# Seven block products for eight in half of an attention's input projection

## The chip, the cores and the metric

The kernel runs on one core of one Trainium2 chip. The core has five engines with instruction streams of their own: TensorE (PE, matmuls), VectorE (DVE), ScalarE (ACT), GpSimd (POOL) and SyncE (SP, which here only issues transfers). Sixteen DMA engines move data between the chip's memory and the core's buffers: SBUF (128 partitions) and PSUM (8 banks of 512 fp32 numbers for each partition, into which PE writes). The metric is the device time of one execution in microseconds.

## The reference

A diffusion step of two layers over 256 prompt tokens and 2048 sample tokens (a grid of 32 rows by 64 columns) of width 1024. Layer 0 is a convolution branch, layer 1 neighbourhood attention with 16 heads of 64:

```python
for i in range(DEPTH):                       # 2 layers
    shift, scale, gate = ada_params(c, ada_w[i], ada_b[i])
    h = modulate(x, norm_g[i], shift, scale) # RMS norm, scaled and shifted
    if i % 2 == 0:
        out = conv_branch(h, conv_w_in, conv_dw_w, conv_dw_b, conv_ln_g, conv_ln_b, conv_w_out)
    else:
        q, k, v, z = split(h @ na_w_in, 4)   # the input projection: 1024 x 4096
        att = attention(q, k, v, ...)        # prompt: its own keys; sample: 8 x 16 window + 512 cached keys
        out = (att * silu(z)) @ na_w_out
    x = x + gate * out
y = rms_norm(x, final_g)                     # also the prompt's k and v are outputs
```

Everything is fp32 in and out. The kernel keeps the accuracy by splitting each operand in a high and a low part in the PE's reduced format (hi = rounded, lo = rest) and adding three products: hi x hi, hi x lo and lo x hi.

## The kernel before

**Stages.** `conv_layer` runs layer 0's input projection and convolution; `conv_out_pipeline` and `conv_out` its output projection, tile by tile of 128 tokens, and store `x1_d`. Then layer 1's input projection goes in two sets of tokens: A (prompt 256, sample 0 to 767) and B (sample 768 to 2047, as blocks of 256, 512 and 512). `na_rest` makes q, k and z (`part` 0, 1, 3): one *pass* for each of 8 column tiles `ct` and 3 parts loads a weight of 1024 x 128, splits it (`halves`: ACT rounds, POOL subtracts) and multiplies each block of the set, 8 k-tiles by 3 matmuls (`project`, L362 to L364). `na_values` makes v with 256 columns a time, 128 tokens a time (L1009 to L1011). Results go to memory: `qh_d`, `ql_d`, `ks_d`, `vs_d`, `zn_d`. `phase2` is the attention of the sample tokens by units of a head, 512 queries and one of four column blocks (names `sa_`); it reads them back.

**Side work** that depends on no product is woven in among the passes: `context_keys` and `context_values` (cached keys and values split in parts), `masked_bias` (for 16 heads and 3 kinds of row, a tile of three slices, mask minus bias, stored to `bm_d`; DVE at L1105, store at L1106), `gated_weights` (the output weights times the gate, split), `prompt_attention`, `prompt_out`. `weave(main, side, n)` takes n side steps after each step of the main work:

```python
self.weave(self.na_values(B, lambda: next(rest)), side, 2)     # side: context keys, masked bias
self.weave(itertools.islice(rest, 13), side, 3.6)
...
self.weave(itertools.islice(rest, 6), side, 13)                # prompt attention, gated weights, context values
...
self.weave(itertools.islice(rest, 2), side, 18)                # prompt output
```

**Order.** In the convolution, and on PE and DVE in the attention, instructions stay in the program's order. In between, a planner orders each engine's instructions by a simulated timeline, with the program's order as priority; on the chip each engine then runs its own list in that fixed order and waits by semaphores. Tiles come from pools by tag with a number of buffers; a new tile waits until the last readers of its buffer are done. When a pool closes, its memory goes to a later pool, under the same rule.

**Hand-over.** The last passes of set B are interleaved by hand with the first scores of the attention (`self.begun`, banks in `s0`), whose loads `start_attention` issues earlier.

## Time and profile before

| what | value |
|---|---|
| median of 3 runs (lowest, highest) | 2794.38 us (2789.11, 2807.89) |
| the profiled execution | 2795.33 us |
| its span, first to last instruction | 2793.5 us |
| mean granted clock of TensorE in it | 0.992 |
| busy: PE, DVE, ACT, POOL | 2679.9, 1766.0, 1377.9, 1408.2 us |
| bytes moved | 533.86 MB, mean 191 GB/s |

In the profile's rows a tile is named as in the program with its numbers left out: `ni_s` is the PSUM bank of a pass over sample tokens, `nip_`/`nis_` weights of set A and B, `v_ps` and `wv_` those of the values, `h_s_hi` the high part of the input, `bm` a tile of the bias. L362 is a line of the kernel. "<-" after an idle time names what ended it. SPq is the queue of transfers that SP issues; a granted clock of 1.00 is full speed. Busy times of PE include the tails of overlapping matmuls. The stretches of the work: output of the convolution from about 745 us, passes of set A to 1220, values of set A to 1330, values of set B to 1441, passes of set B to 1826, the attention to the end.

### The profile page before, as it was taken

To read this page: it belongs to the slowest core of one execution; us is meant where nothing else is said; L and a number is where in the kernel's file an instruction comes from. 1 tells how busy PE (TensorE), PEld (TensorE's weight loads), DVE (VectorE), ACT (ScalarE), POOL (GpSimd) and SP (SyncE) were. 2 spreads that over 40 slices of the span, in tenths; PEclk is the share of its full clock that TensorE was granted. 3 is DMA by queue.
4 is the path that set the end of the run, shared out by engine and by line. 5 is a ranking of instruction groups with operands and counts; after the bars stand their busy time and mean duration, and the time that the engine had idled before them with its cause. 6 is when DMAs were issued, how large, how long until landed. Compare 5 with 4: busy or idle time off the path is not lost.

```text
span 2793.5 us, 45263 instructions
## 1 busy us (share of the span) xinstructions
PE 2679.9 (96%) x16081; PEld 2318.9 (83%) x16081; DVE 1766.0 (63%) x3052; ACT 1377.9 (49%) x2437; POOL 1408.2 (50%) x1589
## 2 busy tenths in 40 slices
PE   6999999999999999999999999988999999999998
PEld 4888877776777889999998888777888898888887
DVE  4678778888985510012556532468787787878885
ACT  4446454456453322234222244356676676667774
POOL 4687776567563343355123235244455555555564
PEclk9999999999999999999999999999999999999999
DMA  7233554556546554446789986588666767966652
GB/s 259 72 128 112 179 193 141 163 190 200 176 117 178 161 162 132 127 146 198 244 297 337 365 255 188 190 222 223 201 199 196 203 171 203 275 182 192 197 165 107
DMA packets 443833, 533.86 MB, mean 191 GB/s; under 512 B 77745, under 2 KB 320393, under 8 KB 443480
## 3 DMA queue, kind: packets, MB, share of 16 engines
q1 hardware_dynamic: 435568, 503.82, 59.7%
q10 hardware_dynamic: 6664, 22.82, 2.1%
q0 software_dynamic: 1376, 4.33, 0.4%
q8 instruction: 128, 2.10, 0.3%
q14 instruction: 97, 0.79, 0.1%
HBM read 355.14 MB, written 179.79 MB: 191 GB/s over the span
## 4 chain that ended last, share of the span: by engine, by line
PE 72%; DMA 10%; DVE 5%; POOL 3%; SPq 3%; ACT 3%; issue 3%; POOLq 0%; ACTq 0%; DVEq 0%
PE sa_T L1652 7%; PE ci_ps L362 6%; PE ci_ps L363 6%; PE ci_ps L364 6%; PE sa_O L1681 5%; PE sa_O L1676 4%; PE ni_s L362 4%; PE ni_s L363 4%; PE ni_s L364 4%; PE sa_S L1620 3%; PE sa_S L1619 3%; DMA bm_d<-bm 2%; PE o L1781 2%; PE o L1783 2%; PE o L1782 2%
## 5 line engine op out<-in xcount | busy, mean ns | idle before, releaser
L1646 POOL TENSOR_SCALAR sa_p<-sa_p,sa_m 128x992 f32<-128x992 f32 (+2 forms) x256 | 278.2, 1087 | 428.9 <-DVE sa_m L1645 291.7
L514 POOL TENSOR_TENSOR cv_p<-cv_p,cv_p 128x640 f32<-128x640 f32 (+1 forms) x240 | 359.7, 1499 | 118.7 <-ACT cv_p L511 105.8
L1661 ACT CAST sa_pt<-sa_T 128x512 fp32r<-128x512 f32 (+3 forms) x512 | 275.2, 588 | 207.9 <-PE sa_T L1652 194.5
L113 DVE TENSOR_TENSOR sa_pt<-sa_T,sa_pt 128x512 fp32r<-128x512 f32 (+3 forms) x512 | 328.4, 683 | 12.8 <-ACT sa_pt L1661 12.5
L362 PE MATMUL ci_ps<-h_s_hi,ci_wh 128*128 128x512 f32 x768 | 307.6, 400 | 9.1 <-ACT z L481 3.6
L364 PE MATMUL ci_ps<-h_s_hi,ci_wl 128*128 128x512 f32 x768 | 303.7, 395 | 0.0
L363 PE MATMUL ci_ps<-h_s_lo,ci_wh 128*128 128x512 f32 x768 | 303.7, 395 | 0.0
L1644 ACT ACTIVATE sa_p<-sa_S,sa_m 128x992 f32<-128x992 f32 (+2 forms) x256 | 267.3, 1044 | 66.8 <-DVE sa_m L1640 59.5
L1652 PE MATMUL sa_T<-ident,sa_p 128*128 128x128 f32 (+3 forms) x2048 | 272.9, 276 | 17.0 <-DVE sa_pt L113 16.9
L1652 PEld LDWEIGHTS sa_T<-ident,sa_p 128*128 128x128 f32 (+3 forms) x2048 | 237.6, 138 | 54.5 <-issue 14.8
L1638 DVE TENSOR_REDUCE sa_m<-sa_S 128x1 f32<-128x512 f32 x256 | 176.2, 688 | 146.3 <-PE sa_S L1620 133.4
L511 ACT ACTIVATE cv_p<-u,ws 128x640 f32<-128x640 f32 (+1 forms) x256 | 190.9, 777 | 134.7 <-DVE u L478 98.4
L534 DVE SCALAR_TENSOR_TENSOR cv<-u,dw,cv 128x640 f32<-128x640 f32 (+1 forms) x240 | 196.2, 817 | 0.5
L1681 PE MATMUL sa_O<-sa_pt,a_v 120*128 120x256 f32 (+5 forms) x1280 | 190.2, 278 | 0.0
L362 PEld LDWEIGHTS ci_ps<-h_s_hi,ci_wh 128*128 128x128 f32 x768 | 145.6, 190 | 49.1 <-ACT z L481 6.8
L534 DVE SCALAR_TENSOR_TENSOR cv<-cv_d,dw,cv 128x640 f32<-128x640 f32 (+1 forms) x224 | 182.8, 816 | 0.0
L1676 PE MATMUL sa_O<-sa_pt,cv 128*128 128x256 f32 x1024 | 174.9, 293 | 5.0 <-ACT sa_pt L1661 1.1
L1640 DVE CUSTOM_DVE_ANT_0 sa_S<-sa_S,a_bm,sa_m 128x480 f32<-128x480 f32 (+2 forms) x256 | 170.9, 668 | 11.3 <-DMA a_bm<-bm_d 2.4
L364 PEld LDWEIGHTS ci_ps<-h_s_hi,ci_wl 128*128 128x128 f32 x768 | 145.5, 189 | 33.6
L363 PEld LDWEIGHTS ci_ps<-h_s_lo,ci_wh 128*128 128x128 f32 x768 | 145.7, 190 | 31.1
L1681 PEld LDWEIGHTS sa_O<-sa_pt,a_v 120*128 120x128 f32 (+2 forms) x1280 | 166.8, 190 | 0.0
L362 PE MATMUL ni_s<-h_s_hi,nis_wh 128*128 128x512 f32 x384 | 150.3, 391 | 2.7 <-ACT ni_s_f L1047 2.4
(808 smaller groups left out, 7121.5 us busy)
## 6 DMA issues: line engine op xcount, KB each, us to landing
adaw<-in_ada_w SPq DMA_DIRECT2D x24, 1024.0 KB
ci_w<-in_conv_w_in SPq DMA_DIRECT2D x48, 512.0 KB
a_bm<-bm_d SPq DMA_DIRECT2D x32, 720.0 KB
x_s<-in_x_sample SPq DMA_DIRECT2D x32, 512.0 KB
vs_d<-v_s SPq DMA_DIRECT2D x128, 128.0 KB
a_qh<-qh_d SPq DMA_DIRECT2D x128, 128.0 KB
a_ql<-ql_d SPq DMA_DIRECT2D x128, 128.0 KB
a_v<-vs_d SPq DMA_DIRECT2D x32, 480.0 KB
```

The source lines that it names most:

```text
L113: self.nc.vector.tensor_tensor(out=lo, in0=src, in1=hi.bitcast(F32), op=ALU.subtract)
L362: self.nc.tensor.matmul(out, wh[:, k, :], hh[:, k, :], start=k == 0, stop=False)
L363: self.nc.tensor.matmul(out, wh[:, k, :], hl[:, k, :], start=False, stop=False)
L364: self.nc.tensor.matmul(out, wl[:, k, :], hh[:, k, :], start=False, stop=k == NK - 1)
L514: nc.gpsimd.tensor_tensor(out=st["t", 0], in0=st["t", 0], in1=st["t", j], op=ALU.add)
L534: nc.vector.scalar_tensor_tensor(out=st["acc", b], in0=d, scalar=w, in1=st["acc", b], op0=ALU.mult, op1=ALU.add)
L1644: nc.scalar.activation(p[:, n], S[:, n], AF.Exp, scale=-1.0, bias=m[:, 2:3], accum_out=m[:, 3:4])
L1646: nc.gpsimd.tensor_scalar(out=p[:, n], in0=p[:, n], scalar1=m[:, 3:4], scalar2=1.0, op0=ALU.mult, op1=ALU.mult)
L1652: nc.tensor.transpose(t[:w, c * P : c * P + P], p[:, x + c * w : x + c * w + w], self.ident)
L1661: nc.scalar.copy(pt[:w, 0, part, :, at], t)
L1676: nc.tensor.matmul(o, cv[:, c].rearrange("p s d -> p (s d)"), x, start=s + c == 0, stop=False)
L1681: nc.tensor.matmul(dst, v[:w, c0 + c].rearrange("p s d -> p (s d)"), loc[:, lo:hi], start=False, stop=s == 1 and c == 3)
```

## The change

Sample tokens 1024 to 2047 leave the pass scheme. Their input is one matrix, split in two halves of 512 tokens and two halves of 512 inputs; a pair of weight tiles is split likewise. The product of two 2 x 2 block matrices is made from seven block products (Winograd's form of Strassen's scheme) instead of eight, with sums of blocks before and after. The sums of input blocks are made once (`input_sums`: factors 11, T1, T2, 22, T3, 21, T4), the sums of weight blocks for each pair (`weight_sums`), the sums of products as they come (`combine`). `in_turn` makes weights ahead for `AHEAD` = 7 products (3 in the value groups).

The first set becomes prompt 256 and sample 0 to 1023, the last 256 of them as a *late block* of its own: it joins after the first value pass, and its passes for `ct` 0 and 1 and its first values come last (`end`). Prompt passes for `ct` 4 to 7 come first, alone (`alone`). All side work is put beside this set by `along`, which takes side steps by tokens done. The bias is stored slice by slice, its masks are kept in bf16; weight loads of the passes are issued by ACT, stores of the bias and the values by SP as before (the values' by ACT in the last group). Prompt output stays beside the block products. The attention begins after the last product, with nothing of it begun before.

```diff
+AHEAD = 7
+PARTS = 1, 0, 3
+BIAS_RATE = 2.0
+SIDE_RATE = 0.5
...
+    def along(passes, n, *sides):
...
+            for i, (side, rate) in enumerate(sides):
+                due[i] += rate * m / P
+                while due[i] >= 1:
+                    next(side, None)
+                    due[i] -= 1
...
+    def input_sums(self, blocks, pool, rows, h):
...
+        yield from rounded("11", b11, False)
+        yield from rest("11", b11)
+        yield from minus(b11, b12, b11)
+        yield from rounded("T1", b11, False)
+        yield from rounded("22", b22, True)
+        yield from minus(b12, b22, b12)
+        yield from rest("22", b22)
+        yield from minus(b22, b22, b11)
+        yield from rest("T1", b11)
+        yield from rounded("T2", b22, False)
+        yield from rounded("21", b21, True)
+        yield from rounded("T3", b12, False)
+        yield from rest("21", b21)
+        yield from minus(b21, b21, b22)
+        yield from rest("T2", b22, "b11")
+        yield from rest("T3", b12, "b22")
+        yield from rounded("T4", b21, False)
+        yield from rest("T4", b21, "b12")
...
+    def in_turn(self, groups):
+        todo = [(g, i) for g in groups for i in range(7)]
+        made, loaded, live = [], 0, 0
+        def load(upto):
+            nonlocal loaded
+            while loaded < min(upto, len(groups)):
+                next(groups[loaded]["w"])
+                loaded += 1
+        load(1)
+        for at, (g, i) in enumerate(todo):
+            while len(made) < len(todo):
+                j = len(made)
+                cost = todo[j][0]["cost"]
+                if j > at and live + cost > self.ahead:
+                    break
+                load(j // 7 + 1)
+                made.append(next(todo[j][0]["w"]))
+                live += cost
+                if j % 7 == 6:
+                    load(j // 7 + 2)
+            w, made[at] = made[at], None
+            g["product"](i, w)
+            live -= g["cost"]
+            yield
...
+        def put(f, i, half):
+            self.rest_out(cts[i], part, t0 + half * n, f, f"{nm}_{i}{half}")
+        def product(i, w):
+            pm = self.product_bank(f"{nm}_{i}")[:, :n]
+            wh, wl = w
+            hh, hl = h[FACTORS[i]]
+            for k in range(4):
+                nc.tensor.matmul(pm, wh[:, k, :], hh[:, k, :], start=k == 0, stop=False)
+                nc.tensor.matmul(pm, wh[:, k, :], hl[:, k, :], start=False, stop=False)
+                nc.tensor.matmul(pm, wl[:, k, :], hh[:, k, :], start=False, stop=k == 3)
+            tile = lambda tag: self.ws.tile([P, n], F32, tag=tag, name=f"{nm}_{tag}", bufs=2 if tag in ("s1", "u2") else 1)
+            self.combine(i, pm, kept, tile, put, scale)
+        kept = {}
+        return {"w": self.weight_sums(srcs, [P, 4, P], pool, nm), "product": product, "cost": 1}
...
+                t = kept["u2"] = tile("u2")
+                join(t, kept["s1"])
+                u4 = kept["u4"] = tile("u4")
+                nc.gpsimd.tensor_tensor(out=u4, in0=t, in1=kept["s5"], op=ALU.add)
+            elif i == 3:
+                join(kept["u4"], kept["u4"])
+            elif i == 4:
+                u3 = kept["u2"]
+                join(u3, u3)
+                nc.gpsimd.tensor_tensor(out=kept["s5"], in0=kept["s5"], in1=u3, op=ALU.add)
+            elif i == 5:
+                join(kept["s1"], kept["s1"])
+            else:
+                join(kept["u2"], kept["u2"])
+        done = {3: ("u4", 0, 1), 4: ("s5", 1, 1), 5: ("s1", 0, 0), 6: ("u2", 1, 0)}.get(i)
+        if done:
+            put(kept.pop(done[0]), *done[1:])
...
+    def masked_bias(self, heads, bufs, rows):
...
             nc.sync.dma_start(raw, self.bias_rows(h))
             for gk, G in enumerate((0, 1, 3)):
                 r0, R = KEY_ROWS[G]
                 view = lambda ap: ap[:, : 32 * R].rearrange("p (a r c) -> p a r c", a=4, c=CW)
-                t = work([P, 3, 480], "bias", 3, f"bm{gk}_{h}")
                 for i, cb in enumerate((16, 8, 0)):
+                    t = work(f"bm{gk}{i}_{h}")
                     bv = self.windows(raw, b0 * BIAS_COLS + cb, R)
-                    nc.vector.tensor_tensor(out=view(t[:, i]), in0=view(masks[gk][:, i]), in1=bv, op=ALU.subtract)
-                nc.sync.dma_start(self.bm_d[h, gk, :, :, : 32 * R], t[:, :, : 32 * R])
-                yield
+                    nc.vector.tensor_tensor(out=view(t), in0=view(masks[:, gk, i]), in1=bv, op=ALU.subtract)
+                    nc.sync.dma_start(self.bm_d[h, gk, :, i, : 32 * R], t[:, : 32 * R])
+                    yield
...
+            own = [(part, ct, A[:], "a") for part in PARTS for ct in range(2)]
+            alone = [(part, ct, A[:1], "p") for ct in range(4, NK) for part in PARTS]
+            first = own[:1] + [x for i in range(1, 6) for x in (own[i], *alone[2 * i - 2 : 2 * i])] + alone[10:]
+            values = [("v", c, A if c else A[:], "a") for c in range(4)]
+            then = [(part, 2 * pair + i, A if pair < 3 else A[1:], "+") for pair in (1, 2, 3) for part in PARTS for i in range(2)]
+            then = [(part, ct, A if ct < 4 else A1, "+") for part, ct, _, _ in then]
+            last = []
+            todo = first + values + then
+            end = [(part, ct, last, "+l") for part in PARTS for ct in range(2)] + [("v", 0, last, "l")]
+            products = self.passes(todo + end)
+            self.along(products, len(first), (out, 0.22))
+            for _ in out:
...
+                side = self.layer1_block(*late_block)
+                self.along(products, 1, (side, 0.8))
                 for _ in side:
                     pass
+                A.append(late_block)
+                A1.append(late_block)
+                bias = self.masked_bias(range(NH), 4, self.xp)
+                side = itertools.chain(self.context_keys(), self.gated_weights(), self.context_values())
+                beside = (bias, BIAS_RATE), (side, SIDE_RATE)
+                self.along(products, 3, *beside)
+                pq = prompt.enter_context(tc.tile_pool(name="pq", bufs=2, side="right"))
+                pqs = prompt.enter_context(tc.tile_pool(name="pqs", bufs=1, space=bass.MemoryType.PSUM, side="right"))
+                pa = map(bool, self.prompt_attention(pq, pqs))
+                self.along(products, 12, *beside, (pa, 0.22))
+                for _ in itertools.chain(bias, side):
+                    pass
+            hbf = c.enter_context(tc.tile_pool(name="hbf", bufs=1))
+            with tc.tile_pool(name="extra2", bufs=1) as xp:
+                self.xp = Tagged(xp, {"ln": 5})
+                side = self.input_rows(FIRST_SUMMED, hbf, blocks)
+                self.along(products, 1, (pa, 0.3))
+                self.along(products, 5, (pa, 0.3), (side, 1.25))
+                for _ in itertools.chain(side, pa):
+                    pass
+            prompt.close()
+            late.close()
+            right = lambda name: tc.tile_pool(name=name, bufs=1, side="right")
+            quarters = c.enter_context(ExitStack())
+            hb = quarters.enter_context(right("hb"))
+            self.xp = None
+            side = self.input_sums(blocks, hb, hbf, summed)
+            self.along(products, None, (side, 2))
+            for _ in side:
+                pass
...
+            more.close()
+            self.more = None
+            banks.close()
...
+                self.pm[:] = [(pool, bufs)]
+            self.ahead = AHEAD
+            with ExitStack() as s:
...
+                products = self.in_turn(self.rest_sums((FIRST_SUMMED, summed), self.x2))
+                side = self.prompt_out(po, pps)
+                self.weave(itertools.islice(products, 7), side, 0)
+                self.weave(products, side, 0.85)
...
+                self.ws = s.enter_context(tc.tile_pool(name="wv", bufs=1))
+                product_banks(s, "pv", 3)
+                products = self.in_turn(self.value_sums((FIRST_SUMMED, summed), self.x2))
+                for _ in range(4):
+                    next(products)
+                self.tail = True
+                for _ in products:
+                    pass
+            quarters.close()
             self.start_attention()
...
-            self.more = self.s0 = None
+            self.first_loads()
 
 
```

`input_rows` reads `x1_d` again, normalises and transposes it into the blocks b11, b12, b21, b22. `weight_sums` loads the two (values: four) weight tiles, gives high and low parts of a11, s1 = a21 + a22, s2 = s1 - a11, s4 = a12 - s2, s3 = a11 - a21, a12, a22 in this order; ACT rounds, POOL subtracts (DVE for s4, in the value groups for s2 and s3 too). `rest_out` splits q and k and stores them with z. Loads of the first two heads are issued by `first_loads` after the last products in the program's order, those of their values and gates by `load_rest` in the attention.

More of the change, by code (lines that the diff above doesn't have):

```diff
@@ L79, in __init__ @@
         self.ctx = ctx
[L80 removed]
         self.tail = False
[L82 removed]
+        self.pm, self.turn, self.later = [], 0, []
+        self.more, self.more_turn = None, 0
+        self.prompt_tiles = 0
         self.cp = ctx.enter_context(tc.tile_pool(name="consts", bufs=1))
@@ L966, in spread_bias, with rest_sums, value_sums @@
+    def rest_sums(self, block, pool):
+        todo = [(pair, part) for pair in range(NK // 2) for part in PARTS]
+        return [self.rest_group(*block, pair, part, pool) for pair, part in todo]
+    def value_sums(self, block, pool):
+        return [self.value_group(*block, g, pool) for g in range(2)]
     def spread_bias(self):
@@ new lines, in values @@
+    def values(self, _, c, w, src, t0, n, hi, lo):
+        nc = self.nc
+        wh, wl = w
+        for s in range(0, n, P):
+            pm = self.mm_bank(f"v_ps{c}_{src}{t0 + s}")[:, :256]
+            for k in range(NK):
+                h = hi[:, k, s : s + P]
+                nc.tensor.matmul(pm, h, wh[k], start=k == 0, stop=False)
+                nc.tensor.matmul(pm, h, wl[k], start=False, stop=False)
+                nc.tensor.matmul(pm, lo[:, k, s : s + P], wh[k], start=False, stop=k == NK - 1)
+            self.store_values(c, src, t0 + s, pm)
+            yield P
@@ L1065, in store_values @@
+    @staticmethod
+    def along(passes, n, *sides):
+        due = [0] * len(sides)
+        while n != 0:
+            m = next(passes, None)
+            if m is None:
+                break
+            if m == 0 and n:
+                n -= 1
+            for i, (side, rate) in enumerate(sides):
[3 more added lines that the diff above has]
+                    due[i] -= 1
     def store_values(self, c, src, t0, pm):
```

639 lines of the change are left out of this document (400 added, 239 removed).

## Prediction

> **What bounds the kernel now.** I read the page's head first.
>
> ```profile
> span 2793.5 us, 45263 instructions
> PE 2679.9 (96%) x16081; PEld 2318.9 (83%) x16081; DVE 1766.0 (63%) x3052; ACT 1377.9 (49%) x2437; POOL 1408.2 (50%) x1589
> ```
> TensorE is busy 96% of the span. The profiled execution took 2795.33 us, 1.8 us around its span; the median of the three runs is 2794.38 us, so the two are used as one, and times below are sums from 2795.33. One per cent, 28 us, is about what a measurement of this kernel can tell from no change.
>
> The change lies between the convolution and the attention, so the second view is the table by stretch: output of the convolution with the first set's projections (900 to 1220), first set's values, second set's values, nine passes of the second set beside the bias, prompt attention, prompt output, hand-over to the attention. Columns after the length: PE, PEld, DVE, ACT, POOL, granted clock, DMA share, GB/s.
>
> ```profile
> 900.00:1220.00 320.00, 320.00 (x1966) 283.91 (x1965) 63.72 (x77) 79.24 (x142) 122.82 (x100) 1.00 0.50 146
> 1220.00:1330.00 110.00, 108.02 (x924) 107.62 (x923) 32.95 (x64) 47.56 (x97) 63.96 (x89) 1.00 0.59 190
> 1330.00:1441.00 111.00, 107.64 (x904) 106.80 (x903) 56.14 (x102) 26.52 (x57) 19.55 (x14) 1.00 0.83 267
> 1441.00:1606.00 165.00, 161.88 (x840) 138.71 (x839) 99.32 (x137) 42.47 (x69) 49.94 (x31) 1.00 0.98 340
> 1606.00:1700.00 94.00, 92.14 (x537) 81.33 (x537) 30.74 (x51) 43.11 (x104) 42.65 (x55) 1.00 0.85 254
> 1700.00:1800.00 100.00, 98.80 (x523) 84.66 (x522) 37.23 (x60) 34.77 (x64) 29.03 (x36) 1.00 0.50 159
> 1800.00:1850.00 50.00, 39.05 (x222) 33.83 (x221) 19.20 (x42) 17.26 (x33) 19.74 (x28) 0.90 0.86 242
> ```
> From 900 to 1800 PE is busy 886.6 of 900 us at a granted clock of 1.00: work taken from PE is time. But a busy PE hides short gaps, because the shown matmul durations overlap; the real price is the step from start to start, in the timeline:
>
> ```profile
> 1800.17 0.39 PE L364 MATMUL ni_s<-h_s_hi,nis_wl 128*128 128x512 f32 x1
> ...
> 1804.94 0.39 PE L364 MATMUL ni_s<-h_s_hi,nis_wl 128*128 128x512 f32 x1
> ...
> 1379.87 0.28 PE L1009 MATMUL v_ps_s<-wv_s_wh,h_s_hl 128*128 128x256 f32 x1
> ...
> 1383.27 0.28 PE L1009 MATMUL v_ps_s<-wv_s_wh,h_s_hi 128*128 128x256 f32 x1
> ```
> The first two rows lie 21 matmuls apart: 0.227 us for one of 512 columns. The last two lie 30 apart: 0.113 us for 256 columns, in the values. The table shows a second limit: from 1441 to 1606 the DMA engines are at 0.98 while PE is at 98%, so both end together there. Third, the SP queue in the same stretch:
>
> ```profile
> 1500.24 0.37 SPq L1130 DMA_DIRECT2D qh_d<-ni_s_h  x1
> ...
> 1529.51 0.49 SPq L1216 DMA_DIRECT2D w_d<-w_50t  x1
> ```
> Thirty-five transfers begin from the first of these rows to the last (grouped rows counted in full), 29.3 us apart: 0.84 us each, nearly without a pause. The last row is a store of the gated weights, whose turn in the program comes only after the bias: work is moved up where an engine is free.
>
> **The change, part by part.**
>
> *Products.* For 1024 sample tokens and a pair of weight tiles, eight block products become seven, each of 4 k-tiles by 3 matmuls. For q, k and z there are 12 groups (4 pairs by 3 parts): 12 x 12 = 144 matmuls of 512 columns go, 144 x 0.227 = 32.7 us. For the values there are 2 groups, and one product is 48 matmuls of 256 columns: 96 go, 96 x 0.113 = 10.9 us. Sum **-43.6 us**, all on PE. Nothing else on PE changes in number: the prompt passes done alone and the late block of 256 tokens are the same matmuls at another time; they only load their weights twice. The convolution's output now goes beside 18 short passes, at a slower pace than in the row 900:1220, where PE never idles; nothing is counted for it.
>
> *Sums and joins in the block stage.* Prices:
>
> ```profile
> L110 POOL TENSOR_TENSOR nis_wl<-nis_w,nis_wh 128x1024 fp32r<-128x1024 f32 x24 | 59.7, 2493 | 125.0 <-ACT nis_wh L354 103.8 <-PE v_ps_s L1011 12.6 <-DMA ks_d<-ni_s_h 5.0
> L110 POOL TENSOR_TENSOR ni_s_l<-ni_s_f,ni_s_h 128x512 fp32r<-128x512 f32 x24 | 32.3, 1345 | 9.0 <-DMA ks_d<-ni_s_h 3.2 <-DMA ks_d<-ni_s_l 2.4 <-DVE bm L1105 1.8
> L762 DVE TENSOR_TENSOR ln_s_z<-ln_s_v,ln_s_z 128x1024 f32<-128x1024 f32 x15 | 18.7, 1250 | 10.9 <-ACT ln_s_v L756 10.9
> L1221 DVE TENSOR_TENSOR po_t<-po_raw,po_gate 128x512 f32<-128x512 f32 x16 | 10.9, 690 | 21.6 <-DMA po_raw<-in_na_w_out 21.4
> L354 ACT CAST nis_wh<-nis_w 128x1024 fp32r<-128x1024 f32 x24 | 25.0, 1047 | 23.9 <-DMA nis_w<-in_na_w_in 10.7 <-PE ni_s L363 10.3 <-DMA ks_d<-ni_s_h 2.8
> ```
> A group of q, k or z has 84 steps of PE, 19.1 us. POOL subtracts six low parts (1.35 us each) and makes two additions: 10.8 us; q adds four low parts: 16.2. DVE has four weight sums and one low part at 0.69, five joins and, for keys, four low parts: at most 9.7 us. ACT rounds seven factors and keeps two products, about 8 us. None reaches 19.1, so I cost these at nothing, hidden under PE; if POOL's cover in the q groups goes, it is 2 or 3 us for each of four groups. A value group has 38 us of PE against about 15 of POOL and 22 of DVE. I take 5 us for the whole block stage; bounds 0 and 32 (the locks, below).
>
> *Input sums.* 24 DVE instructions of 128x1024 at 1.25 us are 30 us, with ACT's rounds (1.05 us) in the chain: the first factor is ready 2.1 + 2.5 = 4.6 us after the rows, the second at about 17, the last at about 34. They have to wait until the last pass of the first set has let go of its input blocks, whose memory they take. Beside them PE has only the late block's seven passes: six of 24 x 0.113 = 2.7 us and one of 5.4, 22 us. Products then want a factor every 2.7 us. If the rows are there in time, that leaves PE waiting some 5 us. The first group's weights share four buffers with the late block, so their loads start only when its last pass ends: a load, a rounding and a subtraction, 5 to 8 us, partly the same wait. Together I take 10 us; bounds 0 (prompt output, 22 us of PE, fills it) and 34.
>
> *Sides.* All side work now lies before the sums. These are its transfers before; weight, bias and cache bytes stay what they were:
>
> ```profile
> bm_d<-bm SPq DMA_DIRECT2D x16, 720.0 KB
> bm_d<-bm SPq DMA_DIRECT2D x16, 576.0 KB
> bm_d<-bm SPq DMA_DIRECT2D x16, 528.0 KB
> w<-in_na_w_out SPq DMA_DIRECT2D x8, 512.0 KB
> cvs_d<-cv SPq DMA_DIRECT2D x8, 512.0 KB
> rb<-rpb_d SPq DMA_DIRECT2D x16, 241.0 KB
> mask<-in_nb_mask SPq DMA_DIRECT2D x3, 720.0 KB
> ck<-in_cache_k SPq DMA_DIRECT2D x4, 512.0 KB
> kc_d<-ck_h SPq DMA_DIRECT2D x16, 128.0 KB
> kc_d<-ck_l SPq DMA_DIRECT2D x16, 128.0 KB
> cv<-in_cache_v SPq DMA_DIRECT2D x4, 512.0 KB
> w_d<-w_00h SPq DMA_DIRECT2D x1, 256.0 KB
> w_d<-w_71t SPq DMA_DIRECT2D x1, 256.0 KB
> ```
> Stores of the bias are 16 x 1824 KB = 29.9 MB; with rows, masks, context keys (2.1 + 4.2), gated weights (4.2 + 8.4, from 32 stores) and context values (2.1 + 4.2), 61 MB. To it come the first set's own weights (18 passes of 512 KB and four of 1 MB, 13.6) and outputs (values 10, q, k and z 17), prompt attention 11.5 and rows 4.2: 117 MB from the first value pass to the sums. At 340 GB/s, the row 1441:1606, that is 345 us. PE in that stretch, by the steps above: value passes 22 + 3 x 27.1, six passes of 24 x (0.227 + 3 x 0.113) = 13.6 and, without the prompt, twelve of 10.9, transposes and prompt attention 25: 341 us. So DMA and PE end together, as from 1441 to 1606, where PE lost 3.1 of 165 us. Before, these sides had the 370 us from the first bias instruction (1328.1, next row) to 1700.
>
> The bias is also cut finer: 144 stores where there were 48, each queued on SP.
>
> ```profile
> L1105 DVE TENSOR_TENSOR bm<-mask,rb x144: 511/554/2856, 1328.1 to 1612.3; 128x352 f32<-128x352 f32 x48, 128x480 f32<-128x480 f32 x48, 128x384 f32<-128x384 f32 x48
> L1106 SPq DMA_DIRECT2D bm_d<-bm x48: 396/608/3310, 1331.5 to 1615.3; - x48
> ```
> A bias instruction has a median of 0.55 us, and one issue of its store 0.61. Ninety-six more issues are 58 us of SP. I count 560 SP issues in the stretch: bias with rows and masks 169, other sides 89, prompt attention 72, values 78, q, k and z 142, rows 10. Weight loads have left SP for ACT's queue, where a load behind a blocked rounding would be late, but two buffers lie ahead. SP's need is bounded by 0.61 us and by 0.84 us each: 342 to 470 us against PE's 341, plus 22 of the late passes. [...] Behind a blocked store on SP stand the stores of keys and values, whose six buffers PE's results need.
>
> *Hand-over.* Two units of attention were begun among the last products; now none are.
>
> ```profile
> 1816.52 0.47 PE L1619 MATMUL sa_S<-ck,a_qh 128*128 128x512 f32 x1 [2.93 <-DMA a_bm<-bm_d]
> ...
> 1821.85 0.99 POOL L1646 TENSOR_SCALAR sa_p<-sa_p,sa_m 128x864 f32<-128x864 f32 x1 [4.44 <-DVE sa_m L1645]
> ...
> 1837.53 1.76 PE L1652 MATMUL sa_T<-ident,sa_p 128*128 128x128 f32 x7 [7.54 <-DVE sa_pt L113]
> ```
> Before, PE waited 2.9 us for a load and 7.5 us for DVE. After, the first loads lie over memory that the last group lets go of factor by factor, so they land early, but the chain of the first unit (scores at 1816.52 to the end of its scaling on POOL at 1822.84, 6.3 us) is bare. One wait replaces the other: 0, bounds -8 and +10.
>
> *Recovered.* PE's idle time from 1220 to 1441, 2.0 + 3.4 us, came from rows of the second set and from context keys beside values; I count -5.
>
> Sum: -43.6 + 5 + 10 - 5 = -34: 2795.3 - 34 = **2761 us**.
>
> **Rivals.**
>
> *More is won*: the sides start earlier, nothing waits at the sums, the hand-over gains 8. -43.6 - 5 - 8 + 2 = -55: about 2741. For it: the gated weights' early store above. Against: it needs a DMA rate above 340 GB/s for 340 us.
>
> *The sides end late*: queue and DMA engines, at 82 to 90% of the rate taken, need 383 to 421 us of PE's 363, and rows and sums, which take the sides' memory, follow with their 10; PE idles 30 to 68 us ahead of the first block product. -43.6 + 5 - 5 + 49 = +5: about 2800. For it: the row of the bias among the waits,
>
> ```profile
> DVE bm L1105 <- DMA bm_d<-bm: 43.1, 23, 4.9
> ```
> 23 waits already at the slower pace of before. Against: the products themselves went on there.
>
> *Slower*: PE itself falls into the pace of the side transfers. Bias instructions stand in DVE's fixed order between the low parts of keys and values; one that waits for its buffer's store holds them, PSUM stays full, and PE stops. It decides from the point at which the planned order asks for more than 340 GB/s. At the rates of the diff (two bias pieces and half a side step for 128 tokens' worth of PE, 2.7 us) bias and sides end after 197 us; their 61 MB with 26 of products and prompt attention are 87 MB, 256 us at 340 GB/s: +59, and the 15 above: 2795.3 - 43.6 + 74 = 2826 us or more. Against: in 1441 to 1606 sides fell behind without PE.
>
> *Locks in the block stage*: the maximum of the bias instruction, 2856 ns over a median of 554, is 2.3 us longer, about one POOL subtraction of 2.49. If DVE's weight sums stand behind POOL like this once in each of 14 groups with the chain of sums exposed, 14 x 2.3 = 32 us: 2793. [...]
>
> **How the numbers follow.** Forecast 2761 (2748 to 2776): 0.43. More won: 0.14. Sides late: 0.26. Slower: 0.12. Locks: 0.05. Faster by over 1% is below 2766: two thirds of the first, the second, a little of the third: 0.45. Slower, above 2822: 0.11. Within: 0.44. The range reaches from the second case to the late sides, 2738 to 2816, and leaves out most of the slower one.
>
> **What would show it.** Right: 144 and 96 matmuls fewer, PE's busy time lower by their share; DMA near 1 for some 340 us before the first block product; PE idle there 10 to 15 us; POOL below PE in the block stage. Wrong: DVE's bias waiting for its store for much more than 43 us with PE idle behind it; a long wait of the first block product for the sums; a bare stretch over 20 us ahead of the first transposes of the attention.

## The result, and the profile after

The change made the kernel slower: 2923.88 us (median of four runs, 2916.88 to 2930.80) against 2795.08, a ratio of 1.045 (95% interval 1.041 to 1.050). Forecast was 2761, with a range up to 2816. The profiled execution took 2930.80 us, 135.5 more than the one of before, and its mean granted clock was 0.965 where it had been 0.992.

The head of the page after the change:

```profile
span 2929.0 us, 45486 instructions
PE 2712.9 (93%) x15841; PEld 2330.2 (80%) x15841; DVE 1931.1 (66%) x3191; ACT 1461.7 (50%) x2595; POOL 1520.3 (52%) x1623
```
The 240 matmuls are gone (16081 to 15841), and yet PE's busy time rose by 33 us. Busy time holds stretched matmuls too, so the table by stretch has to be read with its clock column (same columns as before; output of the convolution with the short passes, side stage, rows and input sums, block products, hand-over):

```profile
745.00:1110.00 365.00, 325.06 (x1678) 273.62 (x1677) 180.92 (x203) 129.34 (x243) 160.63 (x149) 0.94 0.49 139
1110.00:1504.00 394.00, 342.69 (x2317) 319.26 (x2315) 197.95 (x322) 119.91 (x255) 123.34 (x132) 0.91 0.89 284
1504.00:1592.00 88.00, 73.83 (x503) 68.64 (x504) 44.40 (x30) 60.19 (x123) 64.40 (x56) 0.92 0.60 178
1592.00:1936.00 344.00, 340.74 (x1776) 287.90 (x1776) 180.59 (x213) 128.12 (x221) 187.85 (x130) 0.99 0.51 155
1936.00:1968.00 32.00, 5.17 (x16) 3.86 (x15) 5.58 (x12) 4.35 (x8) 0.98 (x1) 0.58 0.76 229
```
Only the block products run at nearly full clock (0.99) and nearly without gaps (PE busy for 340.74 of 344 us), as every stretch from 900 to 1800 did before. Three things catch the eye: the first row is busy for 89% at a DMA share of 0.49; the second reaches a DMA share of 0.89 at 284 GB/s, not 0.98 at 340; the last is bare.

To price the stretches I add up, for each, its matmuls at their full-rate steps and take that from its length: 0.2275 us for 512 columns and 0.1135 for 256 (the trace of before has medians of 0.227 from 1441 to 1606 and 0.113 from 900 to 1220), and 0.06 for a transpose, an estimate from pairs of them, where the second began 0.108 us after the first and the next matmul 0.028 after that. What is left is time **lost** to gaps and to matmuls at half rate. The count has a floor: the block stage, almost without gaps, shows 5%. Its usual steps are 0.233 and 0.118 us, a little over the two figures taken here, and that alone is some 9 of its 16.6 us. (The step of 0.113 that the prediction took for 256 columns is below the medians of both value stages before, 0.118 and 0.120.)

| part | long | lost after | lost before, and where (us of its trace) | difference |
|---|---|---|---|---|
| convolution's output, short passes | 365.4 | 81.8 | 27.7 (745 to 900) + 6.6 (to 1220) | +48 |
| side stage | 393.9 | 96.2 | 9.0 + 10.8 + 4.7 + 5.2 (1220 to 1700) | +66 |
| rows and input sums | 87.6 | 25.7 | none such | +26 |
| block products | 344.1 | 16.6 | 3.4 + 4.3 (1700 to 1828) | +9 |
| hand-over | 31.8 | 29.5 | 8.3 (1828 to 1837.5) | +21 |
| sum | | 249.8 | 80.0 | +170 |

PE's own work came out 39.6 us shorter, the attention 5 us longer: 170 - 40 + 5 = 135, the difference of the two executions.

Of the 250 us, some 50 are the extra time of matmuls at half rate (under 10 before). They come in runs, which in this trace begin within some 3 us after PE restarts from a gap of 0.8 to 7.6 us. The timeline of PE in the side stage (start, length, engine, line, operation, idle time before it):

```profile
1193.26 0.28 PE L1352 MATMUL v_ps_s<-wav_wh,h_s_hl 128*128 128x256 f32 x1
1195.51 0.38 PE L1350 MATMUL v_ps_s<-wav_wh,h_s_h 128*128 128x256 f32 x1 [1.97 <-DVE v_s L127]
...
1196.79 0.28 PE L1351 MATMUL v_ps_s<-wav_wl,h_s_h 128*128 128x256 f32 x1
...
1197.04 0.41 PE L1350 MATMUL v_ps_s<-wav_wh,h_s_h 128*128 128x256 f32 x1
...
1200.02 0.41 PE L1352 MATMUL v_ps_s<-wav_wh,h_s_l 128*128 128x256 f32 x1
1200.23 0.37 PE L1350 MATMUL v_ps_s<-wav_wh,h_s_h 128*128 128x256 f32 x1
1200.44 0.29 PE L1351 MATMUL v_ps_s<-wav_wl,h_s_h 128*128 128x256 f32 x1
```
From 1197.04 to 1200.23 lie 15 matmuls: 0.213 us each instead of 0.118 just before. The wait of 1.97 us is followed, 1.5 us after the restart, by 3.2 us at half rate, which costs another 1.5. Not every such gap is followed by this. Before the change PE had a wait of 2.16 us, and the 7 us from then on were at full clock (the second row here has the columns of the table by stretch):

```profile
1356.34 0.66 PE L1180 MATMUL ck_t<-ident,ck 128*128 128x128 f32 x4 [2.16 <-DVE ck_l L113]
...
1356.00:1363.00 7.00, 6.66 (x56) 6.66 (x57) 4.54 (x11) 1.23 (x3) 0.00 (x0) 1.00 0.88 259
```

Who makes the gaps? PE's waits from 1110 to 1500 (what PE was to do, what it waited for; us, times, longest):

```profile
PE ni_s L379 <- DVE ni_s_l L127: 14.6, 3, 7.0
PE v_ps_s L1350 <- DVE v_s L127: 8.4, 3, 5.9
PE ni_s L379 <- ACT ni_s_f L1381: 8.4, 4, 3.5
PE v_ps_s L1350 <- ACT v_p_f L1416: 3.9, 2, 2.1
PE pa_S L2021 <- DMA pa_ql<-ql_d: 3.2, 1, 3.2
```
PE waits for PSUM banks, which DVE and ACT empty (`ni_s_l`, `v_s` are low parts of results). DVE in turn waits for the bias's buffers, which the stores that SP issues have to leave, and SP waits for DVE's pieces:

```profile
DVE bm L1449 <- DMA bm_d<-bm: 48.8, 38, 5.7
SPq L1450 <- DVE bm L1449: 15.9, 26, 2.1
```

### The profile page after: what moved, and what is told of

Same layout as the page of the kernel before. It is cut to its first block, busy times and chain, and to the rows that moved or that the text cites. A ratio compares the mean times of both kernels' runs of the same rounds, so it can differ in the third digit from the quotient of the medians.

```text
span 2929.0 us, 45486 instructions
## 1 busy us (share of the span) xinstructions
PE 2712.9 (93%) x15841; PEld 2330.2 (80%) x15841; DVE 1931.1 (66%) x3191; ACT 1461.7 (50%) x2595; POOL 1520.3 (52%) x1623
## 4 chain that ended last, share of the span: by engine, by line
PE 69%; DMA 10%; DVE 7%; ACT 4%; POOL 4%; issue 3%; SPq 3%; ACTq 0%; POOLq 0%; DVEq 0%
PE sa_T L2054 6%; PE ci_ps L379 6%; PE ci_ps L381 6%; PE ci_ps L380 6%; PE sa_O L2083 5%; PE sa_O L2078 4%; PE sa_S L2022 3%; PE sa_S L2021 3%; PE ng L1159 2%; PE ng L1158 2%; PE ng L1157 2%; PE o L2183 2%; PE o L2185 2%; PE o L2184 2%; DMA vs_d<-v_s 2%
## 5 line engine op out<-in xcount | busy, mean ns | idle before, releaser
L2046 ACT ACTIVATE sa_p<-sa_S,sa_m 128x992 f32<-128x992 f32 (+2 forms) x256 | 267.0, 1043 | 59.7 <-DVE sa_m L2042 52.3
L2078 PEld LDWEIGHTS sa_O<-sa_pt,cv 128*128 128x128 f32 x1024 | 139.2, 190 | 9.9 <-ACT sa_pt L2063 8.3
```

Of the source, the lines that this page charges most:

```text
L2046: nc.scalar.activation(p[:, n], S[:, n], AF.Exp, scale=-1.0, bias=m[:, 2:3], accum_out=m[:, 3:4])
L2078: nc.tensor.matmul(o, cv[:, c].rearrange("p s d -> p (s d)"), x, start=s + c == 0, stop=False)
```

## The experiments

Eighteen kernels ran. All but e11 start from the changed kernel, and every ratio is to the kernel before, run beside it on the same chip. "Lost" is the count above, from one profiled execution, by part; the kernels ran on different chips, so for small differences the ratios are safer than the medians. e13, e14 and e18 leave the bias out of the result. In e1, e8, e12 and e16 the side stage also holds twelve short passes that left the first part.

| kernel | us | ratio (95%) | conv. | side | rows, sums | block | hand-over |
|---|---|---|---|---|---|---|---|
| changed | 2923.88 | 1.045 (1.041 to 1.050) | 81.8 | 96.2 | 25.7 | 16.6 | 29.5 |
| e1 short passes in a row | 2894.12 | 1.034 (1.031 to 1.037) | 40.2 | 99.0 | 28.6 | 18.6 | 29.0 |
| e2 lower rates | 2932.51 | 1.048 (1.045 to 1.050) | 84.5 | 99.6 | 27.2 | 18.0 | 30.9 |
| e3 stores by ACT | 2934.18 | 1.049 (1.046 to 1.051) | 81.9 | 93.2 | 30.5 | 17.0 | 28.9 |
| e4 value stores by SP | 2924.10 | 1.044 (1.042 to 1.047) | - | - | - | - | 25.1 |
| e5 seven buffers | 2934.74 | 1.051 (1.046 to 1.055) | 83.6 | 100.2 | 24.7 | 13.9 | 31.4 |
| e6 half the bias late | 2936.01 | 1.051 (1.047 to 1.055) | - | 56.9 | - | 63.8 | - |
| e7 values first | 2915.05 | 1.044 (1.039 to 1.048) | - | - | - | 21.2 | 14.2 |
| e8 = e1, e6, e7 | 2897.93 | 1.037 (1.033 to 1.041) | 37.1 | 74.9 | 23.6 | 59.7 | 19.5 |
| e9 prompt attention later | 2950.86 | 1.055 (1.051 to 1.058) | - | 111.5 | - | - | - |
| e10 = e9, six banks | 2952.93 | 1.056 (1.053 to 1.059) | - | 121.5 | - | - | - |
| e11 before, four banks | 2807.55 | 1.002 (1.000 to 1.004) | | | | | |
| e12 = e1, e7, e10 | 2918.83 | 1.043 (1.040 to 1.047) | - | 133.5 | - | - | - |
| e13 one fixed tile stored | 2952.80 | 1.057 (1.054 to 1.060) | - | 116.3 | - | - | - |
| e14 a quarter stored | 2940.35 | 1.051 (1.050 to 1.053) | - | 99.4 | - | - | - |
| e15 weight loads by SP | 2914.44 | 1.042 (1.041 to 1.044) | 72.7 | 88.1 | 26.0 | 16.7 | 28.7 |
| e16 = e1, e7 | 2892.64 | 1.034 (1.033 to 1.036) | - | - | - | 21.9 | 14.3 |
| e17 a third of the stores | 2939.14 | 1.052 (1.050 to 1.054) | - | 101.2 | - | - | - |
| e18 no bias | 2858.26 | 1.024 (1.021 to 1.026) | 81.1 | 34.4 | 23.8 | 18.0 | 28.5 |

### The convolution's output: e1, e15

```diff
-            first = own[:1] + [x for i in range(1, 6) for x in (own[i], *alone[2 * i - 2 : 2 * i])] + alone[10:]
+            first = own + alone
...
-            self.along(products, len(first), (out, 0.22))
+            self.along(products, len(first), (out, 0.5))
```


> The changed kernel with the six passes of the first set's 1024 tokens beside the convolution's output (two of its tiles for each pass, as before the change), and the twelve passes of the 256 prompt tokens after it in one row. Theory 1, the interleaving is the loss: the short passes leave the norm chain of the next tile without cover, so PE's 60 us of idle and slow steps between 800 and 1110 us fall to the 20 of before: about 2884 us. Theory 2, a pass of 256 tokens can't be fed (2.7 us of PE against load, 1.05 us of rounding and 2.49 us of subtraction) wherever it stands: the idle time moves to the twelve passes, 2915 to 2930 us.

The table by stretch of e1, the convolution's output and then the twelve short passes with the side stage:

```profile
745.00:1018.00 273.00, 257.85 (x1263) 211.34 (x1263) 168.34 (x197) 108.67 (x208) 120.36 (x120) 0.97 0.51 146
1018.00:1467.00 449.00, 390.47 (x2749) 365.05 (x2749) 204.47 (x326) 139.94 (x286) 171.07 (x165) 0.95 0.87 276
```
The clock is back at 0.97 and 42 us less is lost there; the short passes cost a few us where they go, and the profiled time falls by 35, the median by 30. So the cause of this part is shown: it is the prompt passes of 24 short matmuls between the long ones, with the pace of the convolution's output that goes with this order. By which way they cost is less clear. PE's waits for the norms of the convolution's output (`ln_`, 14.3 us in all) fall to 7.5, as they would if the short passes gave too little cover for that chain; but its waits at the prompt passes themselves (`ni_p`: weights being rounded and subtracted, banks) fall as well, from 17 us to 2, and 6.5 us come up again at the head of the next stretch.

In e15 the passes load their weights from SP again (`queue=self.nc.scalar` is dropped).

> The changed kernel with the weight loads of all passes issued by SyncE instead of ScalarE. Theory 1, a load behind a waiting instruction of ScalarE is late and starves the short passes beside the convolution's output: 15 us or more go between 800 and 1110 us, and 5 may come in the side stage: 2905 to 2914 us. Theory 2, the loss there is the norm chain without cover and the time of rounding and subtraction: within 10 us of 2924, or above it by the issues that SP gets in the side stage.

Both stages lose 8 to 9 us less, and the profiled time falls by 18. The median falls by 9 only, within the spread of the changed kernel's four runs (13.9), so this gain is seen in the profile alone. In the changed kernel's trace a load that ACT issued at 1175.41 us came after a rounding that ACT began at 1175.00, having waited 5.38 us for a store of context keys; the prediction named such a delay and counted nothing.

### The side stage: is it the bias, and what of it?

**The bias as a whole (e18).** `bias = iter(())`, and the attention loads the masks in place of the bias, as many bytes.

> The changed kernel without the bias: its subtractions, stores and row loads are left out and the attention loads the masks. Theory 1, the bias is what holds the side stage: 60 us or more of the 83 that PE loses between 1110 and 1500 us go: 2845 to 2865 us. Theory 2, the stage's other crossed work (prompt attention, context keys and values, gated weights, value stores through six buffers) holds PE by itself: 15 to 40 us go, 2885 to 2910 us.

```profile
1105.00:1429.00 324.00, 309.60 (x2271) 291.40 (x2270) 98.77 (x168) 125.83 (x261) 115.03 (x132) 0.98 0.77 239
```
The stage is 70 us shorter (324.1 for 393.9), 34.4 us lost, the clock at 0.98, and the median 66 us lower. PE's waits for DVE at its banks, 23.0 us in the rows above, are all but gone (one row is left of the two):

```profile
PE ni_s L379 <- DVE ni_s_l L127: 0.9, 1, 0.9
```
The bias beside this work, with the rows and masks that it loads, costs 66 us; without it, the other parts are as they were. And this kernel, which makes no bias, is still 2.4% slower than before with its bias.

**Half of it elsewhere (e6).** Heads 8 to 15 are made beside the block products; for the memory, two kinds of kept product there have one buffer instead of two (not shown, nor is `late_bias`).

```diff
-BIAS_RATE = 2.0
+BIAS_RATE = 1.0
...
-                bias = self.masked_bias(range(NH), 4, self.xp)
+                bias = self.masked_bias(range(8), 4, self.xp)
...
-                side = self.prompt_out(po, pps)
+                side = self.mixed(self.prompt_out(po, pps), self.late_bias(range(8, NH), lb), 1.4)
-                self.weave(products, side, 0.85)
+                self.weave(products, side, 1.75)
```


> The changed kernel with the bias of heads 8 to 15 made beside the block products of q, k and z (one row buffer and the mask of one kind at a time; one buffer instead of two for two kinds of kept product, for the memory), and one bias piece for 128 tokens' worth of PE in the first part. Theory 1, the total of the side stage is its price: 15 MB and 80 of its issues move to a stretch where the DMA engines are at 0.57; at 282 GB/s that is 53 us less, and the block products stay at PE's pace: 2870 to 2885 us. Theory 2, something else holds PE there (the order behind PSUM): less than 15 us are won. If the bias disturbs the block stage, that stage is longer than its 343 us by more than 10.

Side stage and block stage of e6:

```profile
1106.00:1452.00 346.00, 316.94 (x2265) 296.94 (x2265) 151.96 (x249) 118.87 (x254) 122.48 (x132) 0.96 0.88 279
...
1548.00:1940.00 392.00, 351.59 (x1776) 292.40 (x1776) 238.87 (x294) 126.19 (x220) 197.40 (x130) 0.96 0.63 195
```
The side stage is 48 us shorter (39 less lost), the block stage 47 longer: DVE has 239 us of work there instead of 181, and PE's longest wait is one of 15.7 us for a join on DVE. The cover of the block products, free by its DMA share (0.51), was not free. That DVE's load is the reason is likely but not shown, since the buffer given up could delay the joins as well.

**Its pace (e2).** BIAS_RATE 2.0 to 1.2, SIDE_RATE 0.5 to 0.3.

> The changed kernel with 1.2 bias pieces and 0.3 side steps for 128 tokens' worth of PE instead of 2.0 and 0.5. Theory 1, PE is held by the order of DVE and SP, which asks for stores faster than they land: with a plan that asks for less, PE loses 40 us in place of 80 between 1110 and 1500 us: about 2884 us. Theory 2, the stores' own throughput ends the stage: the bias ends later by what the plan puts off and the time stays within 12 us of 2924.

```profile
1114.00:1515.00 401.00, 331.70 (x2348) 310.09 (x2347) 192.13 (x325) 131.17 (x268) 128.75 (x140) 0.91 0.89 285
...
1450.00:1500.00 50.00, 14.26 (x89) 12.66 (x87) 32.53 (x60) 9.13 (x20) 5.83 (x10) 0.67 0.93 321
```
Less was lost up to 1450 (50 us for 90), but then some 40 pieces of the bias were left over, and PE stood behind them in one wait of 40.0 us (1469 to 1509), about 1 us a piece. The rate was too low for the passes at hand, so this run can't tell order from throughput; it shows the price of side work that is not done in time.

**Its buffers (e5).** `masked_bias(range(NH), 7, self.xp)` for 4 buffers, paid for by one buffer of `ln`.

> The changed kernel with seven buffers for the bias pieces instead of four (and four row buffers for the side work instead of five, for the memory). 144 pieces took 355 us over four buffers, 9.9 us for one turn of a buffer. Theory 1, the turn of a buffer is the limit (too few stores in flight): the bias ends 100 us earlier and PE's loss between 1110 and 1500 us falls from 80 us to under 40: under 2885 us. Theory 2, the DMA engines' total of some 120 MB at about 300 GB/s is the limit: the bias ends within 20 us of 1490 and the time is within 12 us of 2924.

```profile
DVE bm L1449 <- DMA bm_d<-bm: 9.0, 6, 1.8
```
The wait fell from 48.8 us (38 times) to 9.0 (6 times), and the stage did not move. This wait was the tell that the prediction and my first theory relied on; by itself it is not the limit, unless the row buffer given up took back what the piece buffers won.

**Its queue, its issues, its bytes, its DVE work (e3, e17, e14, e13).** In e3 ACT issues the bias stores; in e17 three slices share a tile and a store, as before the change (with two buffers of three slices for four of one, and one buffer of `ln` less); in e14 `t[:32]` of 128 partitions are stored, and the attention loads the masks; in e13 nothing is subtracted and every store reads one fixed tile.

> The changed kernel with the 144 bias stores issued by ScalarE instead of SyncE. Theory 1, issuing on SP is the limit of the side stage (0.69 us for each of 510 issues from 1150 to 1500 us): 144 fewer free up to 99 us of SP, and 40 us or more go: under 2885 us. Theory 2, the DMA engines or the fixed order behind them are the limit: within 15 us of 2924, and ScalarE's wait for the bias may add to it.

> The changed kernel with the bias stored as before the change, a tile of three slices at a time: 48 stores in place of 144, the same bytes and subtractions (two buffers of three slices for four of one, and four row buffers instead of five, for the memory). Theory 1, the issues on SP and their lag are the price: 96 issues at 0.69 us are 66 us less of SP, and PE's loss between 1110 and 1500 us falls by 30 us or more: under 2895 us. Theory 2, the sum of crossed waits in the fixed orders, of which the number of issues is no part: within 12 us of 2924, above it by the smaller number of buffers.

> The changed kernel with the bias stores cut to 32 of their 128 partitions (a quarter of the bytes and packets, all 144 subtractions and issues; the attention loads the masks instead, so that the bias is left out of it). Theory 1, bytes set the pace: 22 MB less, 65 to 80 us at 282 to 340 GB/s, of which at least 50 are won: 2845 to 2875 us. Theory 2, DVE's work and order, or the number of issues: within 20 us of 2924.

> The changed kernel without the 144 bias subtractions on DVE: every store of a bias piece sends one and the same tile, so that no store waits for DVE and no DVE instruction waits for a store (left out: the bias; its bytes and 144 issues stay). Theory 1, bytes set the pace of the side stage: PE loses 65 to 85 us between 1110 and 1500 us as before, 2910 to 2930 us. Theory 2, the order behind waiting bias instructions does: 40 us or more go, under 2885 us.

None gained; all four took 10 to 29 us longer than the changed kernel. The side stage by stretch in e14:

```profile
1118.00:1508.00 390.00, 333.74 (x2276) 311.30 (x2275) 204.24 (x322) 117.80 (x254) 125.04 (x132) 0.91 0.75 232
```
The DMA engines are at 0.75, and the stage is as long as with 0.89: their throughput isn't the limit by itself. Its waits of DVE and SP:

```profile
DVE bm L1449 <- DMA bm_d<-bm: 24.9, 24, 3.7
SPq L1450 <- DVE bm L1449: 33.1, 44, 2.9
```
SP, whose list has a fixed order, now waits twice as long for DVE's pieces (33.1 us for 15.9); what stands behind each store would wait with it, which these rows don't show. In e13, where DVE makes no pieces, DVE waits for ACT instead:

```profile
DVE pa_pt L127 <- ACT pa_pt L1667: 45.2, 10, 13.5
DVE v_s L127 <- ACT v_s L1423: 35.9, 19, 4.3
```
The second of these waits is as long in e18 (41.7 us, 21 times), where the stage is short, so it is no cause by itself. e13 tells more beside e18: DVE does as much in both (107 and 99 us), the stores and the loads of rows and masks are in e13 alone, and it loses 116.3 us against 34.4. So the transfers of the bias are enough for the loss, without its work on DVE; and by e14 a quarter of the bytes of the stores is enough, with that work.

In e3 the issuing moved, the DMA share was 0.91 at 288 GB/s (0.89 at 284 in the changed kernel) and the stage as long.

**Banks and prompt attention (e9 to e12).** Theory: four PSUM banks for six leave PE no slack. e9 moves the prompt attention behind the bias, e10 also gives its banks to the products, e11 takes two banks from the kernel before (`self.more_bufs = 4` to 2).

> The changed kernel with the prompt attention taken out of the side stage: it begins when bias and other sides are done, beside the last passes (two steps for 128 tokens' worth of PE). The PSUM banks for passes stay four. Theory 1, PE stops in the side stage because four banks, mostly of 256 columns, give results no room while DVE waits for its bias stores: the loss up to the end of the bias stays near 80 us less the 6 us of waits of the prompt attention, and the time is 2910 to 2930 us. Theory 2, the prompt attention's place in PE's order is the loss: 40 us go, under 2890 us.

> As the kernel with the prompt attention moved, with six PSUM banks for passes instead of four while the bias is made (the two banks of the prompt attention are free then). Theory 1, the banks are what PE lacks: its loss between 1110 and 1500 us is halved, 30 to 45 us less than with four: about 2885 us. Theory 2, transfers are the limit whatever PE has room for: the same as with four banks within 12 us.

> The kernel before with four PSUM banks for passes instead of six while the bias and the context keys are made; nothing else is changed. Theory 1, six banks are what kept PE at 98% there though DVE waited 43 us for bias stores: with four it loses 15 to 35 us: 2810 to 2830 us. Theory 2, the banks play no part: 2795 us within 8.

> The changed kernel with three edits that each take one named loss: long passes beside the convolution's output and the short ones after them (30 us measured), six banks while the bias is made with the prompt attention after it (35 expected), value groups first (9 measured). If they are separate: 2850 us (2835 to 2865). If banks do nothing: 2885 us.

The theory fell. e10 loses more than e9. In e11 the stretches of the second set's values and of its passes beside the bias read

```profile
1330.00:1441.00 111.00, 103.80 (x857) 102.79 (x856) 55.86 (x101) 27.03 (x57) 21.97 (x17) 0.98 0.83 265
1441.00:1606.00 165.00, 158.89 (x843) 136.71 (x842) 99.43 (x136) 41.94 (x69) 48.18 (x30) 0.98 0.97 338
```
and the kernel takes 0.2% more (6 us by the ratio, 9 by the medians): that is what two banks are worth there, not 66. The same bias beside the second set's long passes, with four banks too, runs at 338 GB/s. Prompt attention is not the cause either: without it the stage loses 15 us more.

### The hand-over: e4, e7, e16

The waits of PE and ACT there in the changed kernel:

```profile
PE sa_S L2021 <- ACT sa_p L2046: 19.2, 1, 19.2
ACT L2046 <- DMA vs_d<-v_s: 18.1, 1, 18.1
PE sa_S L2021 <- DMA a_k<-ks_d: 7.6, 1, 7.6
```
The first exponential on ACT waits 18.1 us for stores of values, over whose buffers its output lies by the memory plan, and which ACT itself has to issue. Ahead of this the first loads cost 7.6. e4 has SP issue the value stores and puts that output elsewhere:

> The changed kernel with the value stores of the last groups issued by SyncE (ScalarE before) and with the attention's tile p in the memory that the input blocks leave, not over the buffers of those stores. Theory 1, the first exponential waits for the last value stores, which its queue and its memory both stand behind: the bare stretch from 1935 to 1967 us falls by 15 to 22 us: 2902 to 2909 us. Theory 2, the loads of the first heads bound the stretch: 2918 us or more.

The timeline of e4, SP's queue and the first score:

```profile
1894.26 51.86 SPq L1427 DMA_DIRECT2D vs_d<-v_s  x56
...
1953.95 0.77 PE L2020 MATMUL sa_S<-ck,a_qh 128*128 128x512 f32 x1 [18.50 <-DMA ck<-kc_d]
```
One wait took the place of the other: the first loads stand behind 56 stores on SP, and PE waits 18.5 us for them. e7 makes the two value groups ahead of those of q, k and z, and SP issues their stores:

> The changed kernel with the two value groups ahead of the groups of q, k and z, and the value stores issued by SyncE throughout. Theory 1, the bare stretch before the attention (32 us) is the drain of the value stores, which hold ScalarE's queue and the memory of the attention's tiles: it falls to about 15 us, 2905 to 2912 us. Theory 2, it is the landing of the first heads' loads, which start only after the last product in any case: 2918 us or more.

It halves the hand-over, 29.5 to 14.2 us lost (31.8 to 16.7 in length), and the longest wait that is left is for a load: PE's first score reads

```profile
1941.50 0.76 PE L2018 MATMUL sa_S<-ck,a_qh 128*128 128x512 f32 x1 [7.23 <-DMA ck<-kc_d]
```
But the median falls by 9 only, within the spread of four runs (13.9). Together with e1 it adds nothing that can be measured:

> The changed kernel with the two edits that gained: long passes beside the convolution's output with the short ones after them (30 us), and the value groups ahead of those of q, k and z (9 to 15 us). Theory 1, both losses are separate from the side stage: 2879 to 2887 us. Theory 2, the side stage, reached earlier, gives part of it back: 2895 us or more. Either way slower than before.

Against e1 the hand-over kept its gain (14.3 us lost for 29.0), and the earlier parts gave it back: 10 us more are lost ahead of the block products and 3 beside them. e8, with e6's late bias besides, is no better:

> The changed kernel with three edits together: passes of 1024 tokens beside the convolution's output and the short passes after them, the bias of heads 8 to 15 beside the block products, and the value groups first. If the losses are separate, the gains add: 30 measured for the first, 45 and 15 expected of the others, 2834 us (2820 to 2850). If they are one limit (a total of transfers ahead of the sums), the first and second overlap: 2860 us or more.

No kernel here beats the one before; the best of those with the change and the bias, e1 and e16, are 3.4% above it.

## Why the prediction was wrong, step by step

*Products*, -43.6: right. 240 matmuls went, and PE's work fell by 39.6 by count. Two slips in the working change nothing: the busy times from 900 to 1800 add up to 888.5 us, not 886.6, and the rival *locks*, 2793, leaves out the -5 recovered (2789 with it).

*Block stage*, +5: right in size, +9 with the floor of the count. POOL is at 187.85 of 344 us, PE at 340.74. The delay that the rival *locks* priced is there, in the weight sums on DVE (count, busy, mean ns):

```profile
L1086 DVE TENSOR_TENSOR ng_s<-ng_r,ng_r 128x512 f32<-128x512 f32 x11 | 17.0, 1541 | 0.0
```
1541 ns where the page of before has 690 for such an instruction. The group has 12 instructions in the whole stage: five began while no instruction of POOL ran and took 0.68 us each, and seven began while one ran and took 1.77 to 3.56. The matmuls cover it.

*Products*, last sentence: "nothing is counted" for the convolution's output at its slower pace. This failed by **+48**. e1 takes 42 of it away with the interleaving (30 to 35 of the whole time), and e15 takes 9 away with the weights in SP's queue in place of ACT's; the two were not run together, so they may overlap.

*Sides*: failed by **+66**, in both terms. The rate: 340 GB/s was carried over from a stretch in which DMA had long passes beside it; here 284 was reached at a share of 0.89. But the rate didn't set the length: e14 had fewer bytes at 232 GB/s and as long a stage. SP's issues came at 0.73 us each (480 from 1150 to 1500, not the 510 at 0.69 that some expectations name), between the prediction's two ends, 0.61 and 0.84; its sum counts nothing for them, as at the lower end. The cover: I held 341 + 22 us of PE's against 345 of transfers, but the rows take the sides' memory, so all of it has to be done by 1504, within 298 us of PE's work. And "DMA and PE end together" was no model of what came: the DMA share was 0.89 where 0.98 was reached before, and PE was busy for 87% of the stage. PE stops in many gaps of a few us, waiting for the two engines that empty its banks; that these stand in fixed queues with the bias is the likely reason, and in e18 the waits for DVE go with the bias. What is shown: the bias costs 66 us (e18), and half of it makes the stage 48 us longer (e6). What is not: which limit of it. Bytes, issuing queue, banks and DVE work were each taken away alone, the number of issues and the bias's buffers only at the price of other buffers, and the loss stayed. What e13 and e14 have in common and e18 has not are the 144 issues of stores and the loads of rows and masks. Whether two limits have to go together stays open.

*Input sums*, +10: **+26** with the rows, at a clock of 0.92. That this lies within the bounds is partly luck, since the wait came at another place: the first block product waited 3.0 us, and PE's longer waits were for weights of the first set's last passes (7.0 us for POOL, 3.0 for ACT), those of the late block among them.

*Hand-over*, 0 with bounds -8 and +10: failed, **+21**. The first loads didn't "land early": they were issued from 1936.03 on, as the last product ended. And the output of the first exponential wasn't looked up in the memory plan; it lay over the value stores' buffers, queued on the same engine.

```profile
1936.03 1.14 SPq L1967 DMA_DIRECT2D a_qh<-qh_d  x2
...
1963.75 1.28 ACT L2046 ACT_TABLE_LOAD   x1 [18.07 <-DMA vs_d<-v_s]
```
*Recovered*, -5: there was nothing to recover where the whole stretch lost more.

The rival *slower* (2826 or more, at 0.12) had the sign and the picture, PE falling into the pace of the sides; its trigger, the bias waiting for the store of its buffer, isn't borne out by e5; *sides end late* had the rate (83% of the one taken) with PE idle in one place, where the runs show gaps all along. Neither held the convolution's output and the hand-over, 69 us together. Of the tells, the bare stretch ahead of the attention came. The products' long wait for the sums did not (3.0 us). The bias's wait for its store told nothing: 48.8 us after, 43.1 before, where PE ran on at 98%, and 9.0 in e5 for a stage as long.

## What to carry to other kernels

Side work beside matmuls is to be priced against the matmuls that remain until its memory is wanted, and every queue that it shares with the engines that empty PSUM is a suspect; a DMA rate from another stretch isn't carried over without its cover (here 340 GB/s was expected and 284 came). When a stage is made of shorter passes, its gaps can cost more than their length: here some 50 us of slowed matmuls in 250 us lost. A wait that is the longest in the table is tested by taking it away before it is called the cause.

## What the runs showed of the hardware

Some short gaps were followed by matmuls at half rate. After 1.97 us without a matmul, PE ran for 3.2 us at 0.213 us a matmul instead of 0.118 (the rows of the timeline above; the granted clock from 1197.04 to 1200.30 was 0.50), and such stretches make up some 50 of the 250 us lost after the change, against under 10 of 80 before; it is part of why PE's busy time rose with fewer matmuls. The length of one gap doesn't decide it: before the change, waits of 1.79 and 2.16 us in the value stages were followed by no run of matmuls at half rate, and the clock of both stretches was 1.00. What else decides it stays open here.

Of the 12 weight sums above, DVE instructions with two inputs of 128x512 in SBUF, the five that began while no instruction of POOL ran took 0.68 us each, and the seven that began while one ran took 1.77 to 3.56.
